# Two of a projection's column groups: from every eighth token to contiguous token tiles, with the stride moved to the later reads

## The chip, the cores and the metric

The kernel runs on one core of a Trainium2 chip. The metric is the device time of one execution, in microseconds (us), lower is better; times are compared by the median of several runs. The engines are named as in the profile: PE (TensorE matmul), PEld (TensorE's loading of the stationary operand, which overlaps PE), DVE (VectorE), ACT (ScalarE), POOL (GpSimd) and SP (SyncE, which issues most DMAs).

## The reference

Two blocks run one after the other over 1024 tokens of 1024 features. The first (RWKV-7, differential attention, a mixture of experts) is not touched. The second norms its input, multiplies it by one wide weight matrix and splits the columns over three mixers:

```python
h = rms_norm_2(x, pre_norm_w[l])
proj = h @ w_in[l]
z, xbc, dt_raw, q, f_raw, i_in, g, u, s5_gate = jnp.split(proj, splits, axis=-1)
y_ssd = ssd_mixer(z, xbc, dt_raw, ...)
y_hgrn = hgrn2_mixer(q, f_raw, i_in, g, ...)
y_s5 = s5_mixer(u, s5_gate, ...)
mix = jnp.concatenate([y_ssd, y_hgrn, y_s5], axis=-1)
x = x + rms_norm_2(mix @ w_out[l], post_norm_w[l])
```

The change concerns `u` and `s5_gate`, 512 columns each. The S5 mixer is a linear recurrence over time with 32 groups of 16 channels, followed by a gated linear unit; `u` is its input, and `silu(s5_gate)` multiplies its output token by token.

## The kernel before

The normed input of the second block lies in SBUF as `hT` (called `hU` in the rows), feature-major: 128 partitions by 8 blocks of features by 1024 tokens, as a pair of float32r parts, hi and lo. A projection to token-major output is `proj_tm` (L1459): for each chunk of 256 columns it loads and splits the weights (`wh`, `wl`), and for each of 8 tiles of 128 tokens it calls `gemm_tm` (L274), which issues for each of the 8 blocks of features three matmuls (`mm3`, L262 to L264): hi by hi, hi by the weights' lo, lo by hi. The tokens are the stationary operand, 128 by 128, so every matmul has a load of 128 columns of `hT` on PEld before it; the weights, 256 columns, are the moving operand. One `gemm_tm` is 24 matmuls; a projection of 512 columns is 2 chunks of 8 tiles, 384 matmuls. The result goes from PSUM through ACT (L1490, or L1487 with DVE L1488 when a silu is wanted) into a tile `pz` and by an SP DMA (L1470) to DRAM.

Four projections of 512 columns go this way: `I0`, `G0`, `U0`, `SG0`. The first two feed the HGRN mixer and take contiguous tiles, tokens 128 j to 128 j + 127. The last two feed S5, which cuts time into 128 blocks of 8 tokens: they take `tok=eighth`, that is `slice(i, T, 8)`, the i-th token of all 128 blocks. So their stationary operand is read from SBUF with a step of 8 elements (32 bytes), and each result tile is already in the order that S5 wants, one contiguous block of 128 rows of the DRAM arrays `u_d` (block 7 - i) and `g5_d` (block i).

`s5` (L1895) reads `u_d` by 8 DMAs (L1908) of 128 rows of 2048 bytes into a tile `un`, two buffers deep; ACT copies each into `ur` (L1909), and PE transposes `ur` (L1914). Much later it reads `g5_d` the same way (L2003, tile `gs`).

In `mixers` (L2156) `U0` and `SG0` are emitted between the heads of the HGRN mixer: head 0, `U0`, head 1, `SG0`, head 2. The engines' orders are fixed when the kernel is built, by a scheduler that mixes the neighbouring pieces; in the trace the HGRN heads' small matmuls stand among those of `U0` and `SG0` on PE. A head is a chain over seven levels: DVE forms differences (L1547, L1548), ACT takes exponentials (L1549), DVE multiplies (L1550), PE makes the scores (L1555 for three coarse levels, L1566 for four fine ones), DVE merges them into `acc` (L1559, L1567), and so to the next level; then a state recurrence, two products (L1600, L1602), a norm, and transposes (L1613). After the last matmul of `SG0` the memory of `hT` is given back (`es.close()`), and the loads of the following product with `w_out` and of `u_d` can start. The pieces that matter in `mixers`:

```python
eighth = lambda i: slice(i, T, 8)
for h in range(3):
    next(heads)
    if h == 0:
        proj_tm(*a, U0, 512, u_d, tok=eighth, row=lambda i: 7 - i)
    if h == 1:
        proj_tm(*a, SG0, 512, g5_d, silu=True, tok=eighth)
es.close()
```

Of the kernel before, what the change touches and what calls it, by code (L numbers as in the profile page):

```python
# [28 lines left out]
def make_consts():  # L29
    """Constants that depend on shapes alone, one column block each of a [128, n] array."""  # L30
# [57 lines left out]
def flat(ap):  # L88
    """A contiguous DRAM array as one axis."""
    n = 1  # L90
    for s in ap.shape:
        n *= s
    return bass.AP(tensor=ap.tensor, offset=ap.offset, ap=[[1, n]])
# [6 lines left out]
class Parts:  # L100
    """A weight matrix split in hi + lo, in tiles of `part` blocks of 128 rows."""
# [9 lines left out]
class Kern:  # L111
# [19 lines left out]
    def const(self, *names, pool=None):  # L131
        """Load constants to SBUF tiles."""
        out = []
        for nme in names:
            o, n, rows = CONST_AT[nme]
            t = (pool or self.cpool).tile([rows, n], F32, name=f"c_{nme}")
            self.nc.sync.dma_start(t, self.cap[:rows, o:o + n])
            out.append(t)
        return out if len(out) > 1 else out[0]
# [26 lines left out]
    def bcast_row(self, pool, src, n, name, bufs=None):  # L166
        """A DRAM vector on every partition."""
        t = pool.tile([128, n], F32, name=self.name(name), tag=name, bufs=bufs)
        self.nc.sync.dma_start(t, dap(src, 0, [[0, 128], [1, n]]))
        return t  # L170

    def rsqrt(self, out, v):
        """out = v ** -0.5, on [128, few]."""
# [5 lines left out]
    def split(self, hi, lo, src):  # L179
        """src as the sum of two float32r parts."""  # L180
# [3 lines left out]
    def norm_tile(self, pool, x, gain, out=None):  # L184
        """rms_norm of a token tile [128, 1024]."""
# [9 lines left out]
    def transpose_split(self, hi, lo, h, j, nk=8, k0=0, tag="t"):  # L195
        """Token tile j [128, nk*128] -> feature-major hi / lo [128, k, tokens]."""
# [11 lines left out]
    def load_w(self, pool, w, segs, kt=KT, raw_bufs=1, bufs=2, part=4):  # L208
        """Weight columns [kt*128, segs] -> float32r hi, lo, in tiles of `part` row blocks."""
# [18 lines left out]
    def resident_w(self, pool, w, k0, kt, cs, name, raw_bufs=2, gain=None, raws=None):  # L228
        """Row blocks k0..k0+kt-1 of w, columns cs -> Parts in one pair of tiles; a generator, a block at a time,
        that returns it. gain [128, kt]: a factor of every row; raws(k): a tile for the load of a block."""  # L230
# [17 lines left out]
    def finish(self, g):  # L248
        """What the generator g returns."""
# [9 lines left out]
    def mm3(self, out, a, b, first, last):  # L259
        """out += a^T b with a, b split in (hi, lo)."""  # L260
# [5 lines left out]
    def gemm_fm(self, w, c0, n, x, tok0, ntok=512, kt=KT, tag="mm"):  # L266
        """PSUM [n columns, ntok tokens] = (x @ w)^T for weight columns c0..c0+n."""
# [6 lines left out]
    def gemm_tm(self, w, x, j, n, kt=KT, c0=0, tok=None, tag="mm"):  # L274
        """PSUM [128 tokens of tile j, n columns] = x @ w."""
# [14 lines left out]
def rwkv_proj(K, hT, wp, xs_d, pool, order=RWKV_ORDER):  # L290
    """The projected columns after the token shift -> DRAM xs_d [1792, T], feature-major; the decay's part
    through tanh, the output gate's through sigmoid. hT: (hi, lo) of the normed input."""
# [29 lines left out]
def rwkv_core(K, xs_d, o_d):  # L322
    """RWKV-7 branch from its projections; o_d: DRAM [512, T], feature-major."""
# [14 lines left out]
    # by how long a unit needs their tiles  # L338
# [33 lines left out]
    # an array of 8 (pair of chunks, head) x 2 chunks, each [64, 64] and padded to 4160: the rows of one  # L372
    # parity, and the 16 x 16 blocks on all the diagonals (4 * 1040 = 4160)
# [7 lines left out]
    def unit(g, hf, carry):  # L381
        """A half of the tokens of two heads. A generator, that stops before what needs the inverse."""
# [6 lines left out]
        # log decay and its sums inside chunks of 64  # L389
# [13 lines left out]
        # kk = k * k_k, normalised per head  # L403
# [18 lines left out]
        # a, modified k, b = kk * a  # L422
# [7 lines left out]
        # [r~ | a~] and [b~ | k~] per chunk, and the chunk's decay  # L430
# [10 lines left out]
        # bonus: sum of r . k . r_k over a head, times v  # L441
# [7 lines left out]
        # token-major copies; the two chunks of a pair on the two halves of the partitions  # L449
        aP, lr = f4("aP", tag="aP"), f4("lr", tag="lr")       # [a~ | L_ak v], [b^ | L_rb^T]  # L450
# [6 lines left out]
        # scores, transposed: rows (chunk parity, s), per (pair of chunks, head)  # L457
# [14 lines left out]
        # X = (I - L_ab)^-1: 16-blocks by substitution, (chunk, head, block) on the partitions  # L472
# [17 lines left out]
        def blk(lhs, rhs, tag="a"):  # L490
            """Per (pair of chunks, head): lhs^T rhs on both halves, 64 columns."""
# [28 lines left out]
        ah = f4("ah", (128, 8, 128), "ah")     # [A^ | P^]  # L520
# [7 lines left out]
        # per chunk: [G^T | R'^T] and H, heads on the two halves  # L528
# [22 lines left out]
        # y inside the chunks  # L551
# [10 lines left out]
        # chain over the chunks  # L562
# [24 lines left out]
        # group norm per (token, head)  # L587
# [10 lines left out]
        # back to feature-major: (y * ln_w + ln_b + bonus) * g  # L598
# [27 lines left out]
def rope_tables(K, tab_d):  # L626
    """Rotary tables times the gains of q and k -> DRAM tab_d [2, 8, 128, 128]: cosines, signed sines."""
# [15 lines left out]
def proj_diff(K, hT, wp, pool, pd, beside):  # L643
    """The attention's columns -> DRAM pd [T, 1536]. beside(c): a generator of work beside a sixth of them."""
# [13 lines left out]
def norm_rope(K, pool, pd, tab_d, qk_d):  # L658
    """q and k of pd, normed and rotated -> DRAM qk_d [T, 1024]. A generator, by tiles of tokens."""
# [24 lines left out]
def diff_attn(K, qk_d, v_d, o_d, beside):  # L684
    """Differential attention. qk_d: norm_rope's; v_d: DRAM [T, 512]; o_d: DRAM [512, T], feature-major;
    beside: a generator of other work."""
# [4 lines left out]
    # lambda  # L691
# [29 lines left out]
    for i in (1, 2, 3, 4, 5, 6, 7, 0):  # L721
# [5 lines left out]
        # columns: by head, the reciprocals of the two sums  # L727
        rcs = wk.tile([128, 4, 2], F32, name=K.name("arc"), tag="arc", bufs=2)
        for h in range(4):
            # the two softmaxes: their columns of st are maxima, sums, by block of 512 keys  # L730
# [21 lines left out]
            # e0 / s0 - lambda e1 / s1 = (e0 - lambda s0 / s1 e1) / s0  # L752
# [37 lines left out]
def mix(K, o_ds, gate_d, mT):  # L790
    """The sum of the gated branches, feature-major, into mT, by token tile [128, (hi, lo), 8, 128].

    o_ds: the branches' outputs, DRAM [512, T]; gate_d: DRAM [2048, T], tanh of half the gates' logits."""
# [38 lines left out]
def mix_out(K, mT, x, cb):  # L832
    """x1 = x + mixed @ w_out. x: DRAM [T, D]; cb(j, x1) takes every token tile [128, D]."""
# [22 lines left out]
OUT = float(1 << 12)  # past all the rows  # L856
MAXB = 16            # blocks of 128 rows past the first of an expert: at most (2048 - 32) / 128
# [5 lines left out]
def ring_tile(K, ring, *shape, dt=F32):  # L863
    """A tile of 8 KB per partition of the ring that the experts' weights pass through."""
# [3 lines left out]
def moe(K, ring, x1_tiles, y_d, gap, beside, tail):  # L868
    """hierarchical_moe(rms_norm(x1)). x1_tiles(cb) calls cb(j, x) with every token tile x [128, D] of x1;
    ring: the pool of ring_tile; y_d: DRAM [2 T, D], the two parts of the result; gap is a generator of work for  # L870
    the time of the routing, that first emits loads; beside one for the time of the experts; tail() is called
    after the last expert's loads."""
# [7 lines left out]
    tabi = one.tile([128, 2, NE], I32, name="mo_tabi")     # of every slot: the row of its token, of its result  # L880
    nx = one.tile([128, 1], I32, name="mo_nx")
    f1 = lambda n, *s: one.tile([128, *s], F32, name=f"mo_{n}")
    tabf = f1("tabf", 2, NE)                               # the latter, less OUT; its weight
# [11 lines left out]
    with K.pool(name="mo_r", bufs=1) as rp:  # L895
# [16 lines left out]
        def tile_in(j, x):  # L912
# [18 lines left out]
            def top(out, v, m, e):  # L931
                """m: the maximum of v; out: one-hot of its first occurrence."""
# [6 lines left out]
            # softmax over the groups, its top, and the top two experts of that group (the first of equals)  # L939
# [10 lines left out]
            # the rank of every token among its expert's, and the row of the slot table  # L950
# [13 lines left out]
            # the weights  # L964
# [7 lines left out]
            # the rows of the slot table of the experts' first 128  # L972
# [23 lines left out]
        # the number of blocks of 128 rows past the first, by expert  # L996
# [10 lines left out]
        def half(srcs, i, tile):  # L1007
            """Half i of an expert's three weights, by their rows."""
# [16 lines left out]
    def block(idx, dst, wt, raw, x, dyn):  # L1025
        """One block of 128 rows: idx, dst, wt [128, 1], the rows of its tokens and of its results and their weights;
        raw(i): half i of the expert's weights. A generator, that stops before the first products and before the second."""
# [65 lines left out]
    # experts with more than 128 rows  # L1093
    with tc.If(nc.values_load(nx[0:1, 0:1], min_val=0, max_val=MAXB) > 0):
        with K.pool(name="mo_x", bufs=1) as xp:
            f = lambda n, *s: xp.tile([128, *s], F32, name=f"mo_{n}")
            e32, b16 = K.const("e32", "b16", pool=xp)
            # the expert of every further block
# [10 lines left out]
            # the rows of their slot table  # L1109
# [42 lines left out]
class Ple:  # L1152
    """What ple may have done before it: p @ w_ple_proj, a token tile at a time, the first four to DRAM and the
    others to self.tiles; the weights of the gate, with the norm's gain in them."""
# [8 lines left out]
    def loads(self, h):  # L1163
        """Half h of p."""
# [23 lines left out]
    def product(self):  # L1188
        """The next token tile."""
# [45 lines left out]
def ple(K, pp, x1_d, y_d, x3_d, hT):  # L1235
    """x2 = x1 + y; x3 = x2 + sigmoid(rms_norm(x2) @ w_ple_gate) * pp, to DRAM x3_d [T, D];
    hT: (hi, lo) [128, 8, T] of rms_norm(x3), the second block's input."""
    nc, tc, ap = K.nc, K.tc, K.ap
    # by the time of their last use, for what comes next in their place
    with K.pool(name="pl_x", bufs=1) as px, K.pool(name="pl_h", bufs=1) as ph, K.pool(name="pl_w", bufs=1) as wp:  # L1240
# [4 lines left out]
        def first(j):  # L1245
            """x2 of token tile j, half the reciprocal of its root mean square, and its transpose."""
# [42 lines left out]
def ssd(K, hT, wp, pool, zs_d, mixT_d, beside):  # L1289
    """Mamba-2 mixer. hT: (hi, lo) of the normed input, feature-major; zs_d: DRAM [T, 1024], for twice silu(z);  # L1290
    the result goes to rows 0..1023 of mixT_d, DRAM [2048, T], feature-major; beside: a generator of other work."""
# [864 lines left out]
def mixers(K, es, hT, d5, mixT_d, part_d, x3_d, out):  # L2156
# [4 lines left out]
    with K.pool(name="md", bufs=1, space=DRAM) as dd:  # L2161
# [12 lines left out]
        for h in range(3):  # L2174
# [3 lines left out]
            if h == 1:  # L2178
                proj_tm(*a, SG0, 512, g5_d, silu=True, tok=eighth)
# [79 lines left out]
```

## Time and profile before

| | |
|---|---|
| median of 3 runs | 3081.0 us (3079.27 to 3085.3) |
| span of the profiled execution | 3076.1 us (the page gives this for it, and no other time) |
| PE busy | 2897.0 us, 94% of the span |
| PEld busy | 2400.8 us, 78% |
| DVE busy | 1965.6 us, 64% |
| ACT busy | 1319.5 us, 43% |
| TensorE clock granted, mean | 0.964 |

The span runs from the first to the last instruction of one execution. A matmul's busy time in the profile covers its way through the array, and neighbours overlap, so that the distance from one matmul's start to the next one's (called the pitch below) says more than its duration. The clock is a share of full speed: 1.0 is 2.4 GHz, 0.5 is 1.2 GHz. The two changed projections run from about 2505 us to 2737 us of the span.

### The profile page before, as it was taken

Reading aid. Unit: us, or ns where it says so; the run is one execution under the profiler, and the core shown is the slowest. Engines: PE = TensorE matmul, PEld = TensorE weight load, DVE = VectorE, ACT = ScalarE, POOL = GpSimd, SP = SyncE. Lnnn points to the kernel's source line nnn. Section 1 sums busy time; section 2 is a strip of 40 time slices with the busy share of each in tenths; the row PEclk is TensorE's granted clock in tenths of the full one; section 3 lists DMA queues with packets and bytes.
Section 4 is the critical chain, followed back from the end, with each engine's and each line's share of the span. In section 5 each row is a group of like instructions: output and inputs, shape, how many; then the busy total and the mean of one; then the engine's idle time right before and its main releaser. Section 6 shows DMA issues by size and latency. Waiting matters only on the chain. (4 is left out here: it accounts for less than half of the span.)

```text
span 3076.1 us, 47278 instructions
## 1 busy us (share of the span) xinstructions
PE 2897.0 (94%) x18410; PEld 2400.8 (78%) x18410; DVE 1965.6 (64%) x3826; ACT 1319.5 (43%) x2167; POOL 231.9 (8%) x193
## 2 busy tenths in 40 slices
PE   6999999998998989889999997999999999999998
PEld 4888888775776867678777775878988999987776
DVE  4335778644454656679988786688546754548663
ACT  3222223213454222668777775444323343333341
POOL 0000111000000000012121110000000000000000
PEclk9999989997998998999999998999999999999999
DMA  5323333323114455799999995433344442137433
GB/s 162 115 89 82 102 116 107 101 65 106 62 62 144 152 187 195 247 339 378 370 347 335 319 346 212 138 105 95 102 129 128 133 133 74 55 106 232 125 124 127
DMA packets 378145, 503.30 MB, mean 164 GB/s; under 512 B 86039, under 2 KB 234422, under 8 KB 377918
## 3 DMA queue, kind: packets, MB, share of 16 engines
q1 hardware_dynamic: 347742, 458.63, 45.1%
q0 software_dynamic: 11296, 24.57, 2.2%
q10 hardware_dynamic: 18880, 17.05, 1.6%
q8 instruction: 146, 2.39, 0.3%
q14 instruction: 81, 0.66, 0.1%
HBM read 410.26 MB, written 106.68 MB: 168 GB/s over the span
## 5 line engine op out<-in xcount | busy, mean ns | idle before, releaser
L182 DVE TENSOR_TENSOR wh<-we,wh 128x1024 fp32r<-128x1024 f32 x384 | 452.8, 1220 | 72.3 <-ACT wh L181 70.3
L181 ACT ACTIVATE wh<-we 128x1024 fp32r<-128x1024 f32 x384 | 388.5, 1058 | 59.2 <-PE b L264 32.4
L262 PE MATMUL mm<-wh,hU 128*128 128x256 f32 (+1 forms) x768 | 253.3, 332 | 5.3 <-DVE z L1358 4.0
L263 PE MATMUL mm<-wl,hU 128*128 128x256 f32 (+1 forms) x768 | 251.8, 328 | 2.5 <-DVE wl L182 2.4
L264 PE MATMUL mm<-wh,hU 128*128 128x256 f32 (+1 forms) x768 | 250.0, 326 | 0.0
L264 PE MATMUL mm<-wh,hT 128*128 128x256 f32 (+1 forms) x640 | 215.1, 337 | 0.0
L262 PE MATMUL mm<-wh,hT 128*128 128x256 f32 (+1 forms) x640 | 207.0, 341 | 2.4 <-ACT ye L1060 2.3
L262 PE MATMUL mm<-hT,wh 128*128 128x512 f32 x480 | 196.5, 409 | 4.3 <-DVE edge L309 4.2
L182 DVE TENSOR_TENSOR wl<-wr,wh 128x1024 fp32r<-128x1024 f32 (+2 forms) x102 | 116.0, 1139 | 122.6 <-ACT wh L181 113.8
L264 PE MATMUL mm<-hT,wl 128*128 128x512 f32 x480 | 191.9, 400 | 0.0
L181 ACT ACTIVATE wh<-wr 128x1024 fp32r<-128x1024 f32 (+2 forms) x102 | 100.9, 992 | 211.3 <-PE mm L263 156.8
L263 PE MATMUL mm<-hT,wh 128*128 128x512 f32 x480 | 191.5, 399 | 0.0
L262 PEld LDWEIGHTS mm<-wh,hU 128*128 128x128 f32 x768 | 183.0, 239 | 9.6 <-DVE z L1358 5.0
L263 PEld LDWEIGHTS mm<-wl,hU 128*128 128x128 f32 x768 | 184.0, 240 | 5.8 <-DVE wl L182 3.5
L264 PEld LDWEIGHTS mm<-wh,hU 128*128 128x128 f32 x768 | 184.3, 240 | 1.4 <-issue 1.4
L262 PEld LDWEIGHTS mm<-wh,hT 128*128 128x128 f32 x640 | 125.0, 196 | 21.3 <-issue 4.3
L264 PEld LDWEIGHTS mm<-wh,hT 128*128 128x128 f32 x640 | 125.5, 196 | 12.6 <-issue 1.5
L262 PE MATMUL mm<-hU,wh 128*128 128x512 f32 x320 | 128.6, 402 | 4.5 <-ACT wh L181 4.5
L263 PE MATMUL mm<-hU,wh 128*128 128x512 f32 x320 | 127.3, 398 | 0.0
L264 PE MATMUL mm<-hU,wl 128*128 128x512 f32 x320 | 126.7, 396 | 0.0
L263 PE MATMUL mm<-wl,hT 128*128 128x256 f32 x384 | 115.8, 302 | 1.9 <-DVE wl L182 1.9
L262 PEld LDWEIGHTS mm<-hT,wh 128*128 128x128 f32 x480 | 92.3, 192 | 31.4 <-ACT xs L303 4.5
(704 smaller groups left out, 7098.1 us busy)
## 6 DMA issues: line engine op xcount, KB each, us to landing
we<-w_gate SPq DMA_DIRECT2D x64, 1024.0 KB
we<-w_up SPq DMA_DIRECT2D x64, 1024.0 KB
we<-w_down SPq DMA_DIRECT2D x64, 1024.0 KB
wr<-w_in SPq DMA_DIRECT2D x86, 512.0 KB
d_gate<-gz SPq DMA_DIRECT2D x32, 256.0 KB
gt<-d_gate SPq DMA_DIRECT2D x16, 512.0 KB
x<-d_x SPq DMA_DIRECT2D x16, 512.0 KB
dec<-sd_cum SPq DMA_DIRECT2D x16, 512.0 KB
```

The lines of the kernel that those rows point to most:

```text
L181: self.nc.scalar.activation(hi, src, AF.Copy)
L182: self.nc.vector.tensor_sub(lo, src, hi.bitcast(F32))
L262: nc.tensor.matmul(out, a[0], b[0], start=first, stop=False)
L263: nc.tensor.matmul(out, a[0], b[1], start=False, stop=False)
L264: self.last = nc.tensor.matmul(out, a[1], b[0], start=False, stop=last)
```

## The change

`U0` and `SG0` are computed like `I0` and `G0`, from contiguous tiles of 128 tokens, and stored to `u_d` and `g5_d` in the order of tokens; `proj_tm` loses its parameters for other tiles. `s5` reads every eighth row of the two arrays instead of a contiguous block: still 128 rows of 2048 bytes, now 16384 bytes apart in DRAM. The core of the diff:

```diff
-def proj_tm(K, hT, wp, pool, c0, n, dst, silu=False, tok=None, row=None, cs=None):
+def proj_tm(K, hT, wp, pool, c0, n, dst, silu=False):
-            p = K.gemm_tm(w, hT, j, 256, tok=tok(j) if tok else None)
+            p = K.gemm_tm(w, hT, j, CW)
-            r = row(j) if row else j
-            nc.sync.dma_start(dst[r * 128:(r + 1) * 128, c * 256:(c + 1) * 256], z)
+            nc.sync.dma_start(dst[j * 128:(j + 1) * 128, c * CW:(c + 1) * CW], z)
...
+    eighth = lambda a, i: a.rearrange("(n i) c -> i n c", i=8)[i]
-            nc.sync.dma_start(un, u_d[i * 128:(i + 1) * 128, :])
+            nc.sync.dma_start(un, eighth(u_d, 7 - i))
...
-            nc.sync.dma_start(gs, gs_d[i * 128:(i + 1) * 128, :])
+            nc.sync.dma_start(gs, eighth(gs_d, i))
...
-        eighth = lambda i: slice(i, T, 8)
-                proj_tm(*a, U0, 512, u_d, tok=eighth, row=lambda i: 7 - i)
+                proj_tm(*a, U0, 512, u_d)
-                proj_tm(*a, SG0, 512, g5_d, silu=True, tok=eighth)
+                proj_tm(*a, SG0, 512, g5_d, silu=True)
```

`CW` is 256, as before. The rest of the diff removes comments. The built programs have the same instructions in the same order on each engine, with waits on the same semaphores; only addresses and steps differ.

## Rows read from the trace of the kernel before

**Rows 1.** The page, its first line.

```profile
span 3076.1 us, 47278 instructions
```

**Rows 2.** Instructions on tile hU, 2380 to 2444 us (I0): count, ns min/median/max.

```profile
L262 PE MATMUL mm<-wh,hU x128: 277/283/682, 2379.8 to 2443.5; 128*128 128x256 f32 x128
L263 PEld LDWEIGHTS mm<-wl,hU x128: 187/192/192, 2379.8 to 2443.9; 128*128 128x128 f32 x128
```

**Rows 3.** The same view, 2620 to 2742 us (SG0).

```profile
L262 PEld LDWEIGHTS mm<-wh,hU x128: 312/337/344, 2622.3 to 2735.4; 128*128 128x128 f32 x128
L262 PE MATMUL mm<-wh,hU x128: 397/405/517, 2622.4 to 2735.5; 128*128 128x256 f32 x128
```

**Rows 4.** PE in order of time (start, duration), 28 matmuls of I0.

```profile
2399.72 0.28 PE L264 MATMUL mm<-wh,hU 128*128 128x256 f32 x1
...
2402.96 0.28 PE L264 MATMUL mm<-wh,hU 128*128 128x256 f32 x1
```

**Rows 5.** PE in order of time, 23 matmuls of SG0.

```profile
2718.49 0.41 PE L263 MATMUL mm<-wl,hU 128*128 128x256 f32 x1
...
2723.78 0.41 PE L264 MATMUL mm<-wh,hU 128*128 128x256 f32 x1
```

**Rows 6.** PE in order of time, 6 matmuls at the start of U0.

```profile
2510.63 0.44 PE L263 MATMUL mm<-wl,hU 128*128 128x256 f32 x1
...
2511.83 0.44 PE L262 MATMUL mm<-wh,hU 128*128 128x256 f32 x1
```

**Rows 7.** Stretches: length; busy PE, PEld, DVE, ACT, POOL; clock; DMA share, GB/s.

```profile
2508.00:2514.00 6.00, 5.26 (x23) 4.97 (x21) 5.00 (x5) 2.98 (x4) 0.00 (x0) 0.50 0.74 239
2510.60:2601.50 90.90, 90.90 (x551) 90.50 (x550) 51.58 (x71) 34.97 (x44) 2.46 (x2) 0.98 0.20 66
...
2619.80:2688.50 68.70, 68.70 (x488) 67.94 (x487) 42.28 (x67) 25.60 (x32) 2.46 (x2) 1.00 0.16 51
```

**Rows 8.** Stretches, instructions on hU alone: length; PE and PEld busy (count).

```profile
2510.60:2601.50 90.90, 76.88 (x307) 74.52 (x306) 0.00 (x0) 0.00 (x0) 0.98 0.20 66
2601.50:2619.80 18.30, 16.22 (x66) 15.66 (x65) 0.00 (x0) 0.00 (x0) 1.00 0.25 82
2619.80:2688.50 68.70, 51.91 (x203) 49.86 (x203) 0.00 (x0) 0.00 (x0) 1.00 0.16 51
2688.50:2737.00 48.50, 45.91 (x183) 44.32 (x182) 0.00 (x0) 0.00 (x0) 1.00 0.11 36
```

**Rows 9.** Who DVE waited for, 2510.6 to 2601.5: us, times, longest.

```profile
DVE acc L1567 <- PE a L1566: 10.9, 4, 5.7
DVE lv L1547 <- PE a L1555: 10.3, 1, 10.3
...
DVE acc L1559 <- PE a L1555: 5.5, 1, 5.5
```

**Rows 10.** Who DVE waited for, 2619.8 to 2688.5.

```profile
DVE acc L1567 <- PE a L1566: 9.0, 5, 3.2
DVE pz L1488 <- ACT pz L1487: 6.6, 4, 4.7
DVE acc L1559 <- PE a L1555: 5.2, 1, 5.2
```

**Rows 11.** Who DVE waited for, 2688.5 to 2737.

```profile
DVE acc L1559 <- PE a L1555: 11.0, 2, 5.5
```

**Rows 12.** The chain that ended last, in order of time, 2734 to 2746 us.

```profile
2736.18 0.24 PE mm L264
...
2737.31 4.37 DMA fr<-d_mixT
```

**Rows 13.** ACT, then PE, in order of time: the last copy of u, the first transpose.

```profile
2761.91 0.63 ACT L1909 ACTIVATE s_ur<-s_un 128x512 f32<-128x512 f32 x1
...
2778.25 0.60 PE L1914 MATMUL t<-c_ident,s_ur 128*128 128x128 f32 x4
```

**Rows 14.** One stretch, while s5d_ro and s5d_ca are read; columns as in rows 7.

```profile
2786.50:2790.50 4.00, 4.00 (x38) 4.00 (x37) 3.51 (x7) 1.99 (x5) 0.00 (x0) 1.00 0.84 286
```

More of the change, by code (lines that the diff above doesn't have):

```diff
@@ L1456 @@
 LEVELS = (64, 32, 16, 8, 4, 2, 1)
-def proj_tm(K, hT, wp, pool, c0, n, dst, silu=False, tok=None, row=None, cs=None):
+CW = 256
+def proj_tm(K, hT, wp, pool, c0, n, dst, silu=False):
     nc = K.nc
-    for c in cs or range(n // 256):
-        w = K.load_w(wp, K.ap["w_in_2"][0], [(c0 + c * 256, 256)], raw_bufs=2)
+    for c in range(n // CW):
+        w = K.load_w(wp, K.ap["w_in_2"][0], [(c0 + c * CW, CW)], raw_bufs=2)
         for j in range(8):
-            p = K.gemm_tm(w, hT, j, 256, tok=tok(j) if tok else None)
-            z = pool.tile([128, 256], F32, name=K.name("pz"), tag="stage", bufs=3)
-            evac(K, z, p[:, :256], silu)
-            r = row(j) if row else j
-            nc.sync.dma_start(dst[r * 128:(r + 1) * 128, c * 256:(c + 1) * 256], z)
+            p = K.gemm_tm(w, hT, j, CW)
+            z = pool.tile([128, CW], F32, name=K.name("pz"), tag="stage", bufs=3)
+            evac(K, z, p[:, :CW], silu)
+            nc.sync.dma_start(dst[j * 128:(j + 1) * 128, c * CW:(c + 1) * CW], z)
 def proj_fm(K, hT, wp, pool, c0, n, dst, silu=False):
```

## The prediction

> **What bounds the kernel now.** I read the page first: the profiled span is 3076.1 us [rows 1], 4.9 us under the median of the runs, 3081.0. Differences are worked out within the span and taken off the median. Then I looked for what tells the two changed projections from the two that already use contiguous tiles, since all four have the same shapes, weights' source and evacuation. The view of the instructions on tile hU shows it. In I0 a load of the stationary operand has a median of 192 ns and a matmul 283 ns [rows 2]; in SG0 337 and 405 ns [rows 3]. Durations overlap, so the pitch decides, from PE in order of time. In I0 28 matmuls start within 3.24 us, 27 steps of 0.120 us [rows 4]. In SG0 23 matmuls start within 5.29 us, 22 steps of 0.240 us [rows 5]. The granted clock is 1.0, the 2.4 GHz level, in both. The reader is to see that the load, not the product, sets the pitch: the moving operand is the same 256 columns, and a load that takes 145 ns longer goes with a step that is 0.120 us longer.
>
> Is PE what ends last there? The stretches say that PE is busy throughout: 90.90 of 90.90 us and 68.70 of 68.70 [rows 7], while DVE is busy 51.58 and 42.28. DVE's largest waits in the three main stretches are for matmuls [rows 9 to 11]. And what follows waits for the last matmul of SG0: the chain goes from that matmul, at 2736.18, to the DMA issued at 2737.31 into memory that hT had held [rows 12]. So time won before 2737 moves all that follows.
>
> **What the change removes.** The step of 32 bytes in the load of the stationary operand, in 2 x 384 = 768 matmuls. Between 2510.6 and 2737 the rows hold 306, 65, 203 and 182 loads [rows 8]; the other 12 come before. Each gains 0.240 - 0.120 = 0.120 us where the clock is at full speed. At the start of U0 it is not: the clock is 0.50, 1.2 GHz, from 2508 to 2514 [rows 7], and there the stepped matmuls also have a pitch of 1.20 / 5 = 0.240 us [rows 6]. At half the clock the contiguous pitch would be twice 0.120, as an estimate from rows 4, so nothing is won there: the first 12 and, in the 3.4 us from 2510.6, 14 more. That leaves 292, 65, 203 and 182 matmuls. By stretch:
> - A, 2510.6 to 2601.5: 292 x 0.120 = 35.0, so 90.9 becomes 55.9 us.
> - B, to 2619.8: 65 x 0.120 = 7.8, so 18.3 becomes 10.5.
> - C, to 2688.5: 203 x 0.120 = 24.4, so 68.7 becomes 44.3.
> - D, to 2737: 182 x 0.120 = 21.8, so 48.5 becomes 26.7.
>
> If PE stays the bound everywhere, 89.0 us are won.
>
> **What is late next.** The HGRN heads run beside, and their matmuls stand at fixed places of PE's order; PE now reaches them sooner. Take away from A what DVE waits for matmuls: 10.9 + 10.3 + 5.5 = 26.7 us [rows 9]. DVE's own pace, with its work and its waits for ACT and POOL, is then 90.9 - 26.7 = 64.2 us, against 55.9 for PE. In C the waits are 9.0 and 5.2 for matmuls and 6.6 for ACT's evacuation of a projection, which itself waits for PE [rows 10]: 68.7 - 20.8 = 47.9, against 44.3. So in A and C the chain over DVE, ACT and PE and the stream of matmuls come out nearly level, and where two chains that hand over to each other are level, neither runs without waits. What is queued behind a waiting HGRN matmul on PE are the projection's own matmuls, which could have run. A part of DVE's waits for ACT shrinks too, since ACT's exponentials stand behind evacuations that wait for PE; so I take 62 of 64.2 for A, nearer to DVE's pace, and for C 49, just above it. B and D have little DVE work; I leave them at PE's pace. The sum is 62 + 10.5 + 49 + 26.7 = 148.2 instead of 226.4: 78.2 us won. 3081.0 - 78.2 = 3002.8; I say **3003**.
>
> The bounds: at best 89.0, giving 2992. At worst DVE shortens only by its direct waits for matmuls, 26.7 in A, 9.0 + 5.2 in C, 11.0 in D [rows 11], and B by nothing: 51.9, giving 3029.
>
> **What the change adds and moves.** No instruction is added, removed or reordered on any engine. Stores are as many and as large. Every read of u or gate still moves 128 rows of 2048 bytes, now 16384 bytes apart. The nearest row for that step: s5d_ro is read in pieces of 4096 bytes out of rows of 16384, and while it and s5d_ca stream, DMA runs at 286 GB/s over the stretch, its slow start included [rows 14]. I take nothing for the step. The cover, should it cost: u's last copy starts at 2761.91 and its first transpose at 2778.25 [rows 13], 16 us later. The other bound is the rival below. A read also now needs all 16 stores of its array, not two; u's are issued by the end of U0, over 100 us ahead of the first read, and that price is nothing.
>
> **A rule that speaks against it.** Both loads are of 128 by 128, and the stepped one takes 337 ns against 192 [rows 2, 3]. The Trainium skill, page "TensorE: Matmul & The Clock Gate", section "LDWEIGHTS (loading the stationary operand)", gives the time of a load by its number of columns alone, P / 1.2 in ns, an estimate of 107 ns for 128 columns however they are spaced. By that rule the step would be free and nothing won; by the rows 89.0 us are at stake. This trace disagrees with the rule on equal numbers of columns.
>
> **Rivals.**
> 1. The HGRN chain becomes the bound through the whole section. For it: DVE's pace in A, 64.2 us, is above PE's 55.9. Against: B and D hold 247 of the changed matmuls with little beside them. Time: from 3014 to 3029, the lower bound of the gain.
> 2. The longer load is not the step's doing but comes from what runs beside it, and stays: no gain, 3081. Mechanism: DVE's and ACT's traffic on SBUF, or the HGRN matmuls, slow the loads. Against: the 23 matmuls of rows 5 follow one another with no other matmul between, in the quietest stretch, and have the full pitch; the minimum of 312 ns there is above the maximum of 192 in I0 [rows 2, 3].
> 3. The stepped reads of DRAM are slow, and it ends slower than before. Place: u's 8 reads, two buffers deep, whose copies stand in ACT's queue before the last HGRN head's exponentials. To eat 78 us they would have to last 78 + 16 = 94 us more, some 12 us for each of the 8; that is its threshold, and at 24 us each the kernel ends about 100 us slower, near 3180. Against: rows 14. The gate's reads come later and would add to it.
>
> **Chances.** My forecast, PE's pace with 0 to 22 us of new waits (2992 to 3014): 0.73. Rival 1: 0.19. Rival 2: 0.03. Rival 3: 0.02. A still larger gain, from later stretches that fall out better: 0.03. Range 2990 to 3028, from the best bound with 2 us for the spread of the runs to nearly the worst. A measurement of this kernel can tell a change from none at about 0.2%, 6 us: faster 0.95, same 0.03, slower 0.02.
>
> **What would show it.** Loads on hU of about 192 ns and a pitch of 0.120 us through U0 and SG0; the section from 2510.6 to the last SG0 matmul about 148 us long, D about 27; idle of PE before L1566, L1600 and the weights' first matmuls that was not there before, DVE busier than PE in A; the clock still 0.50 only near 2508; reads of u landing as before, and all from the end of SG0 on shifted alike. The prediction is wrong if the loads stay at 337 ns, if A stays above 70 us, if PE's new waits let the clock fall again, or if ACT waits longer for u.

## The result, and the profile after

The changed kernel takes 2987.9 us (2984.9 to 2989.6, 4 runs) against 3081.6 us (3079.3 to 3085.3, 4 runs): a ratio of 0.970, 95% interval 0.9685 to 0.9713, so 88 to 97 us less. The forecast was 3003 with a range from 2990 to 3028: the direction and the source of the gain were right, the gain was larger than forecast, and the time lies 2 us under the range. Compared a second time (the last experiment), the ratio is 0.972, 0.9701 to 0.9736, and the time, 2995.2 us, lies inside the range. The profiled spans are 3076.1 and 2987.4 us, 88.7 apart. The changed kernel's profile is of its slowest run here, 2989.6 us, which is 2.2 us over its span; by the same 2.2, an estimate, the profiled execution of before took 3078.3 us, less than any of its four runs. That accounts for the 5 us between 88.7 and the 93.7 of the medians. In the rows of the changed kernel the lines of the projections' stores and evacuations and of HGRN, L1469 to L1617, are one lower than before (L1565 is L1566 of before).

The loads first. Instructions on tile hU in the second half of the section (end of U0's second chunk, SG0), count and ns min/median/max, which answer to [rows 3]:

```profile
L262 PEld LDWEIGHTS mm<-wh,hU x128: 186/192/193, 2580.2 to 2646.8; 128*128 128x128 f32 x128
L262 PE MATMUL mm<-wh,hU x128: 278/283/387, 2580.2 to 2646.9; 128*128 128x256 f32 x128
```

The load is down from 337 to 192 ns, the matmul from 405 to 283, exactly the values of I0 in [rows 2]. In order of time on PE, 22 matmuls of SG0 start 21 steps of 0.120 us apart ([rows 5] had 0.240):

```profile
2631.71 0.28 PE L264 MATMUL mm<-wh,hU 128*128 128x256 f32 x1
...
2634.23 0.28 PE L264 MATMUL mm<-wh,hU 128*128 128x256 f32 x1
```

The four stretches A to D, cut at the same matmuls as before, then all four; length, then busy PE, PEld, DVE, ACT, POOL, clock, DMA share, GB/s, as in [rows 7]:

```profile
2511.10:2567.30 56.20, 55.86 (x553) 55.25 (x552) 47.36 (x64) 34.50 (x44) 0.81 (x1) 0.97 0.34 106
2567.30:2577.70 10.40, 10.40 (x91) 10.28 (x89) 5.39 (x9) 4.53 (x7) 1.65 (x2) 1.00 0.49 163
2577.70:2621.70 44.00, 44.00 (x488) 43.26 (x488) 38.04 (x63) 24.30 (x31) 2.46 (x2) 1.00 0.24 73
2621.70:2648.10 26.40, 26.40 (x271) 24.85 (x270) 9.82 (x18) 6.14 (x12) 0.00 (x0) 1.00 0.23 76
2511.10:2648.10 137.00, 136.66 (x1396) 133.63 (x1395) 100.61 (x152) 69.47 (x94) 4.92 (x4) 0.99 0.30 94
```

The section takes 137.0 us where it took 226.4, a gain of 89.4. PE at its own pace would have given 55.9, 10.5, 44.3 and 26.7; the stretches came out at 56.2, 10.4, 44.0 and 26.4. The waits that I had added, 62 instead of 55.9 and 49 instead of 44.3, are not there. Who PE waited for, from the first matmul of U0 to the last of SG0 (us, times, longest):

```profile
PE mm L262 <- ACT wh L181: 2.5, 2, 2.2
PE mm L263 <- DVE wl L182: 0.9, 1, 0.9
PE b L1599 <- DVE acc L1566: 0.3, 1, 0.3
```

Only the last row is a wait for the HGRN chain. The other two are for the split weights at the start of U0, ahead of A: 3.4 us, where it was 1.8 before. What follows the section moved as a whole: the last copy of u starts at 2673.25 and its first transpose at 2689.54, 16.3 us apart as in [rows 13], both 88.7 us earlier.

```profile
2673.25 0.63 ACT L1909 ACTIVATE s_ur<-s_un 128x512 f32<-128x512 f32 x1
...
2689.54 0.60 PE L1914 MATMUL t<-c_ident,s_ur 128*128 128x128 f32 x4
```

### The profile page after: what moved, and what is told of

Same layout as the page of the kernel before. It is cut to its first block, busy times and chain, and to the rows that moved or that the text cites. A ratio compares the mean times of both kernels' runs of the same rounds, so it can differ in the third digit from the quotient of the medians.

```text
span 2987.4 us, 47278 instructions
## 1 busy us (share of the span) xinstructions
PE 2806.1 (94%) x18410; PEld 2308.6 (77%) x18410; DVE 1964.4 (66%) x3826; ACT 1318.0 (44%) x2167; POOL 230.2 (8%) x193
## 5 line engine op out<-in xcount | busy, mean ns | idle before, releaser
L262 PE MATMUL mm<-wh,hU 128*128 128x256 f32 (+1 forms) x768 | 224.4, 294 | 6.5 <-DVE z L1358 4.0
L263 PE MATMUL mm<-wl,hU 128*128 128x256 f32 (+1 forms) x768 | 222.7, 291 | 2.5 <-DVE wl L182 2.5
L264 PE MATMUL mm<-wh,hU 128*128 128x256 f32 (+1 forms) x768 | 220.9, 288 | 0.0
L262 PEld LDWEIGHTS mm<-wh,hU 128*128 128x128 f32 x768 | 148.4, 194 | 10.7 <-DVE z L1358 5.0
L263 PEld LDWEIGHTS mm<-wl,hU 128*128 128x128 f32 x768 | 149.2, 194 | 6.0 <-DVE wl L182 3.3
L264 PEld LDWEIGHTS mm<-wh,hU 128*128 128x128 f32 x768 | 149.2, 194 | 1.4 <-issue 1.4
L264 PEld LDWEIGHTS mm<-wh,hT 128*128 128x128 f32 x640 | 124.0, 194 | 12.6 <-issue 1.5
```

Of the source, the lines that this page charges most:

```text
L262: nc.tensor.matmul(out, a[0], b[0], start=first, stop=False)
L263: nc.tensor.matmul(out, a[0], b[1], start=False, stop=False)
L264: self.last = nc.tensor.matmul(out, a[1], b[0], start=False, stop=last)
```

## The experiments

All are edits of the changed kernel, but for two, which edit the kernel before. Two theories stood at the start: the whole gain is the step in the stationary operand's load; or a part of it comes from the stores, the reads or the neighbours. Later ones ask why no waits appeared, and whether the 5 us between spans and medians are a gain made elsewhere.

**The step back in the loads alone, and at other sizes.** `proj_tm` gets a step `s`; the stores go to every s-th row, so that u and the gate stay in token order:

```diff
-def proj_tm(K, hT, wp, pool, c0, n, dst, silu=False):
+def proj_tm(K, hT, wp, pool, c0, n, dst, silu=False, s=1):
...
-            p = K.gemm_tm(w, hT, j, CW)
+            o = j // s * 128 * s + j % s
+            p = K.gemm_tm(w, hT, j, CW, tok=slice(o, o + 127 * s + 1, s))
...
-            nc.sync.dma_start(dst[j * 128:(j + 1) * 128, c * CW:(c + 1) * CW], z)
+            rows = dst.rearrange("(g n r) c -> g r n c", r=s, n=128)[j // s][j % s]
+            nc.sync.dma_start(rows[:, c * CW:(c + 1) * CW], z)
...
-                proj_tm(*a, U0, 512, u_d)
+                proj_tm(*a, U0, 512, u_d, s=8)
...
-                proj_tm(*a, SG0, 512, g5_d, silu=True)
+                proj_tm(*a, SG0, 512, g5_d, silu=True, s=8)
```

With s=8, expected:

> Only the loads of the stationary operand are put back: U0 and SG0 take every eighth token again, and store each tile with every eighth row, so that u and the gate lie in token order and are read with the new step. Theory 1 (the whole gain is the step in the load, and stepped stores and reads cost nothing): loads on hU 337 ns, pitch 0.240 us, time as before, 3081 us within 5. Theory 2 (a part of the gain of 94 us came from the stores or from what the reads trigger): clearly off 3081, by 10 us or more.

Measured: 3081.0 us, ratio to before 1.000 (0.999 to 1.001), although stores and reads are both stepped. From the first matmul of U0 to the last of SG0 it takes 231.1 us, and 231.0 before. So the stepped reads of DRAM, and stepped stores too, cost nothing here that the interval, some 3 us either way, would show, and the loads carry the whole gain: theory 1.

With s=4, expected:

> The same with a step of 4 elements (16 bytes): tile j takes tokens 512 (j div 4) + j mod 4 + 4 n, stored to every fourth row. If a load's time grows with the distance, it lies between 192 and 337 ns, about 250, and the time near 3030 us. If only the crossing to another line counts, it is either as slow as at step 8 (337 ns, 3081 us) or as fast as contiguous (192 ns, 2988 us). The Trainium skill, page SBUF - State Buffer, section Door 1: The DMA port swizzle, names lines of 16 bytes and 4 fp32 as the free stride, but also that two accesses to a line are needed for full speed; at step 4 there is one: the two sentences give 192 and 337.

With s=2, expected:

> The same with a step of 2 elements (8 bytes): tokens 256 (j div 2) + j mod 2 + 2 n, stored to every second row. If time grows with the distance, loads of about 210 ns and a pitch somewhat above 0.120 us, near 3000 us. If only the number of 16-byte lines per access counts, two accesses share a line and the loads stay at 192 ns, pitch 0.120, time 2988 us within 5.

Measured, one run each: 3071.2 us at step 4, nearest to the 3081 of "as slow as at step 8", and 2986.7 us at step 2, within the 5 us of 2988. The loads on hU, in this order step 8, step 4, step 2:

```profile
L264 PEld LDWEIGHTS mm<-wh,hU x194: 336/337/344, 2559.7 to 2734.8; 128*128 128x128 f32 x194
```

```profile
L264 PEld LDWEIGHTS mm<-wh,hU x192: 329/330/334, 2560.0 to 2729.0; 128*128 128x128 f32 x192
```

```profile
L264 PEld LDWEIGHTS mm<-wh,hU x157: 194/195/201, 2561.6 to 2644.2; 128*128 128x128 f32 x157
```

A jump between 2 and 4 elements, 8 and 16 bytes, not a slope: 195, 330, 337 ns; at step 4 the pitch on PE is 0.237 us (17 steps from 2700.07 us). From 4 to 8 elements the cost hardly grows: from the first matmul of U0 to the last of SG0 step 4 takes 226.2 us, step 8 took 231.1. These 5 us are half of the 10 between the two times; the other half is no more than single runs of one kernel differ by. Whether it is the line or the distance that counts, a step of 3 elements would tell; it was not run. The Trainium skill, page "SBUF — State Buffer", section "Door 1: The DMA port swizzle", speaks of lines of 16 bytes and of two accesses to a line for full speed; that sentence agrees with the three medians, while its figure of 4 fp32 as the free step does not: at 4 the load takes 330 ns, and the measurement decides.

**The cost doubled, with other neighbours.** I0 and G0, which run beside the end of the SSD mixer, get the step too:

```diff
-        proj_tm(*a, I0, 512, v_d)
-        proj_tm(*a, G0, 512, gh_d, silu=True)
+        proj_tm(*a, I0, 512, v_d, s=8)
+        proj_tm(*a, G0, 512, gh_d, silu=True, s=8)
```

U0 and SG0 have `s=8` as above.

> The suspected cost doubled: I0 and G0 also take every eighth token and store every eighth row, beside U0 and SG0 as in the first of these runs. Theory 1: another 768 loads at 337 ns, pitch 0.240 us with other neighbours (the end of the SSD mixer); with 768 x 0.120 = 92 us more, 3173 us, less some 5 to 10 us where PE waited there for its weights anyway: 3163 to 3173. Theory 2 (the load's time comes from the HGRN neighbours): loads of I0 and G0 stay near 192 ns and the time at 3081.

Measured: 3165.5 us, ratio 1.027 (1.026 to 1.029), 84.5 us above before and within theory 1's bounds. The loads in the stretch of I0 and G0:

```profile
L264 PEld LDWEIGHTS mm<-wh,hU x203: 312/337/344, 2384.9 to 2559.7; 128*128 128x128 f32 x102
```

They are at 337 ns where they were at 192 [rows 2]. With other neighbours the stepped load takes the same time: rival 2 of the prediction is out.

**A heavier HGRN chain.** The two differences of each level are computed again and written again, so that each level costs DVE more; on the kernel before and on the changed one. The edit for twice (four times has `range(4)`):

```diff
-            nc.vector.tensor_tensor(v4(lv)[:, :, 0], v4(e)[:, :, 0], ref, op=OP.add)
-            nc.vector.tensor_tensor(v4(lv)[:, :, 1], v4(cum)[:, :, 1], ref, op=OP.subtract)
+            for _ in range(2):
+                nc.vector.tensor_tensor(v4(lv)[:, :, 0], v4(e)[:, :, 0], ref, op=OP.add)
+                nc.vector.tensor_tensor(v4(lv)[:, :, 1], v4(cum)[:, :, 1], ref, op=OP.subtract)
```

> The kernel before with a heavier HGRN chain: the two differences on DVE at each of a head's seven levels (L1547, L1548) are computed twice, with the same result. That adds 7 x 1.2 = 8.4 us of DVE work a head, some 21 us in the section of the changed projections and 8.4 us or less for the last head after it. Before, DVE waits 56 us there for matmuls, so both theories expect the section not to grow; the last head may add up to 8: 3081 to 3090.

> The changed kernel with the same addition; its engines have the same order as the run before this one, so the difference of the two is the change's gain under a heavier HGRN chain. Theory W (the prediction's step: DVE's own pace is already the section's, 64 us in the first and 48 us in the third stretch, so that every added us shows): the gain falls from 94 to 77 or less. Theory S (PE paces the section and the chain has room, by the trace after some 8.8 us of idle DVE in the first stretch and 6 us in the third): the gain stays at 85 or more.

> The kernel before with those differences computed four times: 25 us more DVE work a head. DVE's busy time in the first stretch goes from 52 to 77 of 91 us, in the third from 42 to 67 of 69: nearly level there. Both theories: the section grows little, 0 to 10 us; the last head adds up to 25: 3085 to 3115.

> The changed kernel with that addition. DVE's work in the first stretch is then 47 + 25 = 72 us where PE needs 56, in the third 38 + 25 = 63 where PE needs 44. Theory S: DVE becomes the bound, and the gain falls by about 16 + 19 = 35 us, to some 60. Theory W: it falls by the whole 50 us, to some 45. If the gain stays above 80, DVE does not pace the section at all and both are wrong.

| times computed | before | changed | gain | section before | section changed |
|---|---|---|---|---|---|
| 1 | 3081.6 | 2987.9 | 93.7 | 231.0 | 141.3 |
| 2 | 3094.1 | 3011.2 | 82.9 | 229.7 | 144.4 |
| 4 | 3142.6 | 3064.4 | 78.2 | 217.7 | 137.7 |

The section here runs from the first matmul of U0 to the last of SG0. Its rows for the changed kernel, computed twice, then four times (columns as above):

```profile
2510.80:2655.20 144.40, 138.25 (x1349) 134.80 (x1350) 124.28 (x189) 73.15 (x97) 8.36 (x4) 0.98 0.32 103
```

```profile
2509.70:2647.40 137.70, 127.91 (x1202) 124.80 (x1203) 128.91 (x204) 59.25 (x81) 5.56 (x2) 0.95 0.28 90
```

Computed twice, DVE has 20.9 us more work in the section (124.28 against 103.37), and the section of the changed kernel grows by 3.1 us; its gain falls from 89.7 to 85.3, that of the medians to 82.9. Theory W, which wanted 77 or less, falls. Theory S wanted 85 or more: the section's own gain meets it, that of the medians lies 2 us below. Not all of the 3.1 us is the chain's: of PE's 6.3 us of waits in this section (3.7 without the addition) only 0.6 are for pieces of the HGRN heads, the others for weights and for an evacuation, and the clock stands at 0.50 for 6.8 us near the start of U0, where it did for 3.4. A small part of the heads, 40 PE instructions of 1389, also moved behind the section, in both kernels alike.

Computed four times the test is not clean: the scheduler moved a larger part of the heads behind the section (PE instructions there fall from 1389 to 1202, and before's section gets shorter), so that DVE's work in it grew by 25.5 us, not by the 25 us in each of two stretches of the expectation. Both numbers, 60 and 45, missed. What it shows: with DVE busy 128.91 of 137.70 us, 94%, the section still gains 80.0 us. The kernel before ended later than expected with these additions, 4 and 28 us above the two ranges, because the work behind the section grew, in both kernels alike: from 340 us to some 356 and 419.

**The same pair again.** No edit.

> The changed kernel once more, beside the kernel before on one chip, for a tighter difference. The two profiled executions differ by 88.7 us, the medians by 93.7, and the forecast's best bound was 89.0. Theory P (the section's own gain is the 89 us, and the rest is where the executions compared happened to lie in their spread of about 10 us): the difference of the medians comes out between 87 and 92. Theory Q (some 5 us more are really won elsewhere): it stays at 94 or more, and the trace shows a later or earlier stretch that is shorter.

Measured: 2995.2 us (2989.7 to 2998.7, 5 runs) against 3080.0, 84.8 us less, ratio 0.972 (0.9701 to 0.9736, or 81 to 92 us). The section by itself:

```profile
2509.90:2649.80 139.90, 136.49 (x1390) 133.23 (x1390) 103.53 (x154) 73.69 (x98) 4.92 (x4) 1.00 0.34 108
```

It is 139.9 us long, even 1.4 shorter than in the first profile, and its clock is 1.00 throughout: the stretch at half the clock at the start of U0, 3.4 us in the first profile, is missing here. The span, 2993.0, is still 5.6 longer: U0 starts 4.1 us later, and the rest behind the section takes 2.9 us more. So against the one profile of before the section gains 89.7 and 91.1 us in the two, while the difference of the medians comes out at 94 and at 85: that spread does not come from the section. The difference was expected between 87 and 92 by theory P; it came out 2 below that, with an interval that reaches to 92, and theory Q, something won elsewhere, is out.

## Why the prediction was wrong, step by step

**The bound, right.** The load of the stationary operand set the pitch, PE was busy throughout, and what follows waited for SG0's last matmul: 0.240 to 0.120 us of pitch moved everything behind by 88.7 us. One reading beside it was wrong, without consequence: in D the largest wait of DVE was not for a matmul (11.0 us) but for ACT's evacuation of the gate (27.9 us), which itself waited for PE.

**The change part by part, right.** 89.0 us if PE stays the bound; the section gained 89.4. The stepped reads at nothing: held. The half-clock stretch at nothing: about right, for other reasons. In the changed kernel the first 12 matmuls of U0 ran at the full clock, but PE then waited 2.2 us for the weights where it had waited 0.7, and the clock fell only behind this wait; the matmuls at half the clock won a little all the same (last section).

**What is late next, wrong: the failed step.** I took 62 us for A and 49 for C, from a pace of DVE of 64.2 and 47.9. Measured: 56.2 and 44.0, PE's pace. The term of 11 us of new waits was 0.3 us, and DVE was not busier than PE in A, as it was to be. Two things in the trace show why 64.2 was no pace. First, I had taken off DVE's waits for matmuls and kept all the others, 12.6 us in A. But in the changed kernel A's idle time on DVE is 56.20 - 47.36 = 8.8 us, 4.6 of it for matmuls, so 4.2 us are left of the 12.6. Who DVE waited for in A, answering to [rows 9]:

```profile
DVE lv L1546 <- PE a L1554: 2.9, 1, 2.9
DVE lv L1549 <- ACT lv L1548: 2.7, 3, 1.1
DVE acc L1566 <- PE a L1565: 1.7, 1, 1.7
```

The wait for ACT's exponentials halved (it was 5.8 us in A): before, two of those three had stood in ACT's queue right behind an evacuation. The longest of the three waits, 3.1 us, was for the second of these two, behind an evacuation that had waited 5.42 us for PE:

```profile
2590.84 0.39 ACT L1490 ACTIVATE pz<-mm 128x256 f32<-128x256 f32 x1 [5.42 <-PE mm L264]
2591.12 1.05 ACT L1549 ACTIVATE lv<-lv 128x1024 f32<-128x1024 f32 x1
```

I had named that effect and taken only 2 us for it. Second, a stretch cut at PE's matmuls is not closed for DVE. Before, DVE's work in B and D was (third busy number):

```profile
2601.50:2619.80 18.30, 18.30 (x90) 18.20 (x89) 1.47 (x2) 4.53 (x7) 0.00 (x0) 1.00 0.25 82
...
2688.50:2737.00 48.50, 48.50 (x271) 46.98 (x270) 6.44 (x13) 5.20 (x11) 0.00 (x0) 1.00 0.11 36
```

Now it is 5.39 and 9.82, and 47.36 and 38.04 in A and C, where it was 51.58 and 42.28: some 7 to 8 us slid behind PE into B and D, where DVE had been idle. So "nearly level" was wrong too: DVE is at 84% in A, 86% in C and 73% over the section. And even nearer to level, with the chain's differences computed twice and DVE at 86% over the section, it lost 3.1 us, not 11. The levels of the HGRN chain are computed ahead of PE: DVE's last write of a level (L1549) ends 1.5 to 20 us before PE's first matmul on it in the changed kernel, and still 0.3 to 10 us before it with the differences computed twice. So a level that comes a little later costs PE next to nothing.

**The range, too narrow below.** Its low end was the best bound of 89.0 with 2 us for the spread. The runs of the changed kernel alone reach from 2985 to 2999 over the two comparisons, those of before in the first comparison from 3079 to 3085. The section hit the best bound, 89.4 us against 89.0, and the spread of the runs took the rest: that 2987.9 fell under the range and 2995.2 into it is chance. A further slip: the sum came from one profiled execution and was taken off the median of others; the two gains, 88.7 and 93.7, show that this alone can move a forecast by 5 us.

**Rivals.** The HGRN chain as the bound (0.19): out, PE waited 0.3 us for it. A load that is slow for other reasons (0.03): out by the doubled cost. Slow stepped reads (0.02): out, by the first experiment at a ratio of 1.000, and in the changed kernel itself ACT waited 6.5 us for the reads of u, where it had waited 6.3. The rule of the Trainium skill, page "TensorE: Matmul & The Clock Gate", section "LDWEIGHTS (loading the stationary operand)", that the columns alone set a load's time, does not agree with these runs: 192, 195, 330 and 337 ns, all for 128 columns.

## What to carry to other kernels

When the same matmul has two pitches in one trace, compare its weight loads before anything else, and put a stride where it is free: here the rows of a DMA, 2048 bytes each, rather than the elements of a stationary operand. In this kernel a step of 2 fp32 in such an operand cost nothing, and 4 already nearly doubled the pitch. When a bound engine gets faster, don't add a neighbour's idle time to its work as its new pace: ask which of its waits go back to the bound engine through a third one, and whether its work can slide into the next stretch.

## What had not been expected of the hardware

A stepped load kept its time when the clock fell. At 1.2 GHz (2508.2 to 2514.2 us of the kernel before) its median was 337 ns and the pitch 0.240 us [rows 6], both the same as at 2.4 GHz. A contiguous load did not: 192 ns at 2.4 GHz, 330 at 1.2 (2511.5 to 2514.5 us of the changed kernel, clock 0.50). But its pitch was not twice 0.120: there 14 matmuls take 13 steps of 0.213 us, so that a little was won at half the clock too. So a load's duration alone does not give the pitch: with 330 ns it was 0.213 us here, and 0.237 with step 4 at the full clock.

```profile
2511.53 0.41 PE L262 MATMUL mm<-wh,hU 128*128 128x256 f32 x1
...
2514.30 0.41 PE L263 MATMUL mm<-wl,hU 128*128 128x256 f32 x1
```
